# Two key chunks for every query block of the neighbourhood heads, and P transposed by full banks

## Chip, core and metric

The kernel runs on one core of one Trainium2 chip. The metric is device time in microseconds (us) for one execution, the median of the runs shown. Engines: PE is TensorE, DVE VectorE, ACT ScalarE, POOL GpSimd, SP the engine that issues most loads.

## What is computed

A trunk of two layers over 512 tokens of 1024 features, in float32. Each layer projects the normalised input once into queries, keys, values and gates, runs two kinds of attention, gates and projects both, adds the result to x, and adds a SwiGLU block (hidden width 2816). The attention part of a layer, cut:

```
qa, ka, va, qb, kb, vb, ga, gb = split(rms_norm(x) @ w_in)
ya = window_gqa(rope(norm(qa)), rope(norm(ka)), va, sink) @ w_proj_a      # 8 heads, 2 key heads
yb = neighbourhood_attn(norm(qb), norm(kb), vb, rel_bias) @ w_proj_b      # 8 heads
x  = x + (sigmoid(ga) * ya + sigmoid(gb) * yb) @ w_out
```

The **first kind** of head (window) lets a token see tokens at most 128 away, plus a sink in the softmax's sum. The **second kind** (neighbourhood) treats the 512 tokens as a grid of 8 rows by 64 columns. A query sees all 8 rows, and in each row the 16 columns around its own (clipped at the edge), with a bias from a table by row and column distance.

## The kernel before

Matrix products are done in three parts, high by high, high by low and low by high, with every float32 operand split into two float32r halves. PE work comes from two places. The main stream (`layer`, lines 1146 on) issues the projections in order: query, key/value, the second kind's q/k and v, the gates, and from line 1362 the output projections, which first ask for `head15`. Between its matmuls it yields, and a planner (`issue`, `drive`, lines 393 to 419) lets small generators, the chains, issue one step when a model of the engines' clocks says that the step's data will be there. This order is fixed when the program is built. On the chip each engine runs its own instructions in that order, and a step whose data is late holds up all that stands behind it on its engine. All engine calls pass through one helper, so nearly every row of the profile says L309. Scratch tiles come from arenas that a packer fills; a tile can be written only when the tile that lay there before is done with.

Each kind has 8 heads a layer, so 32 heads in all, and each head runs `head` (lines 1010 to 1091):

- For each of four blocks of 128 queries, scores in a bank of 512 columns, "at": one matmul with the high and one with the low half of the keys. Keys are held in four chunks of 128. Block j takes chunks j-1 to j+1 as far as they exist (`span`, `width`), so 256 columns for blocks 0 and 3 and 384 for 1 and 2, ten blocks of 128 by 128 in all. DVE adds mask or bias and finds the maximum, ACT takes the exponential and its sum.
- DVE or ACT scales by the reciprocal of the sum.
- Four steps, one for each key chunk in the order 1, 0, 2, 3 (`CHUNKS`): two or three transposes of 128 by 128 into a bank, ACT copies the high half, DVE subtracts to get the low half, and two matmuls add values times P^T into an output bank. Chunk 1 comes first and opens the bank: its two matmuls run over all 512 columns, with a zeroed last quarter in its buffers (`ptw`, zeroed in `chain_rope_tables`, lines 782 to 802). The other chunks use 256 or 384 columns.

For the second kind tokens are held by column blocks: a block of 128 is 16 grid columns by 8 rows (`by_columns`, `held`), and queries are turned with a reversed identity (`rev`), so that one table slice serves as bias. `chain_pair_b` (lines 1244 to 1271) runs a pair of these heads: `bias_load` issues 8 small loads a head on SP, `q_parts` and `k_parts` turn and split queries and keys, and `k_parts` issues four moves between partitions on SP, two for each head. Then each head waits for its bias, and `bias_mask` adds the mask in three DVE instructions. A pair begins when the bias of the pair before has been added.

Small inputs are issued at the start (lines 707 to 728), x on SP, the rest on POOL: positions, four gain loads, weight slab 1, two gains of the first kind, slab 2, the constants (masks and frequencies), slab 3, the sinks. `first_load` issues slabs 0 to 3 of the query projection. `chain_tables` (lines 744 to 777) first copies positions and negates the sinks on DVE, then uses the constants.

Of the kernel before, what the change touches and what calls it, by code (L numbers as in the profile page):

```python
# [13 lines left out]
F32R = mybir.dt.float32r  # L14
# [5 lines left out]
P = 128  # L20
# [40 lines left out]

C_ID, C_REV, C_MA, C_MB, C_INV, C_W = 0, 128, 256, 640, 752, 784


def constants():

    c = np.zeros((P, C_W), np.float32)
    i = np.arange(P)
    c[i, C_ID + i] = 1.0
    c[i, C_REV + P - 1 - i] = 1.0  # L70
    q, k = i[:, None], i[None, :]
# [3 lines left out]
    qc = 15 - (i % 16)[:, None]  # L75
    kc = np.arange(16)[None, :]
    at = C_MB
    for jb, ds in ((0, (0, 1)), (1, (-1, 0, 1)), (3, (-1, 0))):
        qcol = 16 * jb + qc
        cs = np.clip(qcol - 8, 0, 48)  # L80
        for d in ds:
            kcol = 16 * (jb + d) + kc
            c[:, at : at + 16] = np.where((kcol >= cs) & (kcol < cs + 16), 0.0, NEG)
            at += 16
    c[:, C_INV : C_INV + 32] = np.array(INV_FREQ, np.float32)[None, :]
    return c
# [4 lines left out]
def by_columns(ap):  # L91

    return ap.rearrange("p (r cc c) -> p cc r c", cc=NB, r=8)


def held(ap):
    return ap.rearrange("p (cc r c) -> p cc r c", cc=NB, r=8)

# [115 lines left out]
def trunk(ctx: ExitStack, tc: tile.TileContext, a: dict, out: bass.AP, lay: Layout):  # L214
# [10 lines left out]
    def nm(s):  # L225
        uid[0] += 1
        return f"{s}_{uid[0]}"
# [21 lines left out]
    def act(dtype=F32):  # L249
        return buf([S], dtype)  # L250
# [435 lines left out]
    ident = cst[:, C_ID : C_ID + P]  # L686
    rev = cst[:, C_REV : C_REV + P]
    maskA = cst[:, C_MA : C_MA + 3 * P]
    vec = cp.tile([32, P], F32, tag="vec", name="vec")
# [21 lines left out]
    for c in range(KD):  # L711
        x_load(c)
    posi = cp.tile([P, P], I32, tag="posi", name="posi")
    GQ.dma_start(
        posi[64:68].rearrange("q (r c) -> q r c", c=16), a["positions"].rearrange("(r cc c) -> cc r c", cc=NB, r=8)
    )
    for i, n in enumerate(("q_norm_b", "k_norm_b")):
# [12 lines left out]
    A.copy(warm, ones)  # L730
# [51 lines left out]
    def chain_rope_tables(l):  # L782
        yield Need(keys=["trig"])
        tabs.clear()
        ptw.clear()
        for i in range(4):
            ptw.append(act(F32R))
            V.tensor_scalar(ptw[i][:, 3 * P :], ident, 0.0, None, ALU.mult)
        for i, scale in enumerate((HD ** -0.5, 1.0)):
# [173 lines left out]

    def q_parts(tiles, col, perm, res, scale=None):

        yield Need("pe", tiles, [at_slots])
        ps = turned(tiles, col, perm)
# [37 lines left out]

    ptw = []
    CHUNKS = (1, 0, 2, 3)
    LAST_USE = {0: (0,), 2: (1,), 3: (2, 3)}

    def head(g, q, k, v, bias, perm, init, sink, o_dst, in_a, key):  # L1010

        kh, kl = k
        m = sp.tile([P, NB], F32, tag="negm", name=nm("negm"), bufs=4)
        den = sp.tile([P, NB], F32, tag="den", name=nm("den"), bufs=4)
        pr = []
        for j in range(NB):
            yield Need("pe", [q, kh, kl], [at_slots, sb_slots])
            lo, n = P * span(j)[0], width(j)
            at_slots.take()
            sb_slots.take()  # L1020
            ps = at_bank()
            mm(ps[:, :n], q[:, P * j : P * j + P], kh[:, lo : lo + n], True, False)
            mm(ps[:, :n], q[:, P * j : P * j + P], kl[:, lo : lo + n], False, True)
            sb = buf([3 * P])
            pr.append(sb)
            yield Need("dve", [ps])
            V.tensor_tensor_reduce(
                sb[:, :n], ps[:, :n], bias(j), -1.0, init, ALU.add, ALU.min, m[:, j : j + 1]
            )
            at_slots.give(clock["dve"])  # L1030
            yield Need("act", [sb])
            A.activation(
                sb[:, :n], sb[:, :n], AF.Exp, bias=m[:, j : j + 1], scale=-1.0, accum_out=den[:, j : j + 1]
            )
        done.add(f"{key}scores{g}")
# [8 lines left out]
        for j in range(NB):  # L1044
            n = width(j)
            yield Need("any", [rec])
            if lay.choose(lambda: clock["act"] + 0.2 < clock["dve"]):
                A.activation(pr[j][:, :n], pr[j][:, :n], AF.Copy, scale=rec[:, j : j + 1])
            else:
                V.tensor_scalar(pr[j][:, :n], pr[j][:, :n], rec[:, j : j + 1], None, ALU.mult)  # L1050
        po = None
        for i, c in enumerate(CHUNKS):
            jl, jh = span(c)
            n = width(c)
            yield Need("pe", pr[jl : jh + 1], [at_slots] + ([] if c == 1 else [th_slots]))
            at_slots.take()
            pt = at_bank()
            for j in range(jl, jh + 1):
                x = P * (c - span(j)[0])
                T.transpose(pt[:, P * (j - jl) : P * (j - jl) + P], pr[j][:, x : x + P], perm)  # L1060
            for j in LAST_USE.get(c, ()):
                sb_slots.give(clock["pe"])
            yield Need("act", [pt])
            if c == 1:
                th, tl = ptw[2 * (g % 2)], ptw[2 * (g % 2) + 1]
            else:
                th_slots.take()
                th = buf([3 * P], F32R)
                tl = buf([3 * P], F32R)
            yield from gsplit(pt[:, :n], th[:, :n], tl[:, :n])  # L1070
            at_slots.give(clock["dve"])
            yield Need("pe", [th, tl, v], [at_slots] if c == 1 else [])
            if c == 1:
                at_slots.take()
                po = at_bank()
                o, n = po, S
            else:
                o = po[:, P * jl : P * jl + n]
            mm(o, v[:, c, :], th[:, :n], c == 1, False)
            mm(o, v[:, c, :], tl[:, :n], False, i == NB - 1)  # L1080
            if c != 1:
                th_slots.give(clock["pe"])
        done.add(f"{key}products{g}")
# [9 lines left out]
    def bias_load(l, h):  # L1093

        t = buf([8, 48])
        src = a["rel_bias_b"]
        base = (l * 8 + h) * 15 * BW
        for r in range(8):
            Q.dma_start(
                t[16 * r : 16 * r + 16],  # L1100
                bass.AP(tensor=src.tensor, offset=base + r * BW, ap=[[1, 16], [BW, 8], [1, 48]]),
            )
        return t

    def bias_mask(t):

        bm = buf([7, 8, 16])
        for i, n, d in ((0, 2, 0), (2, 3, -1), (5, 2, -1)):
            m = cst[:, C_MB + 16 * i : C_MB + 16 * (i + n)].rearrange("p (d c) -> p d c", c=16)
            b = t[:, :, 16 * (d + 1) : 16 * (d + 1 + n)].rearrange("p r (d c) -> p d r c", c=16)  # L1110
            V.tensor_tensor(bm[:, i : i + n], b, m.unsqueeze(2).to_broadcast([P, n, 8, 16]), ALU.add)

        def of(j):
            i, n = {0: (0, 2), 3: (5, 2)}.get(j, (2, 3))
            return bm[:, i : i + n].rearrange("p d w c -> p (d w c)")

        return of

# [27 lines left out]
    def layer(l):  # L1146
# [68 lines left out]
        def chain_pair_a(hp):  # L1215
# [3 lines left out]
            qs = []  # L1219
            yield from q_parts(qa, P * hp, ident, qs)  # L1220
            oa.append(act())
# [22 lines left out]
        def chain_pair_b(hp):  # L1244
# [8 lines left out]
            qs, ks = [], []  # L1253
            yield from q_parts(raw, col, rev, qs, scale=gb[:, l : l + 1])
            yield from k_parts(raw, 4 * HD + col, ident, ks)
# [405 lines left out]
```

## Time and profile before

| | |
|---|---|
| median of 3 runs | 1417.02 us (1416.55 to 1417.68) |
| profiled execution, time | 1418.54 us |
| its span, first to last instruction | 1416.8 us |
| PE, DVE, ACT busy | 98%, 66%, 50% of the span |
| mean granted TensorE clock | 0.997 |

Times in the profile count from the start of the span. An engine's busy time is the union of its instructions' durations. A matmul's duration reaches into the next one's, so the mean duration is longer than the distance from one start to the next. Idle time is shown with what released the engine. The granted clock of 1.00 is 2.4 GHz, that of 0.50 is 1.2 GHz.

### The profile page before, as it was taken

To read this page: it belongs to the slowest core of one execution; us is meant where nothing else is said; L and a number is where in the kernel's file an instruction comes from. 1 tells how busy PE (TensorE), PEld (TensorE's weight loads), DVE (VectorE), ACT (ScalarE), POOL (GpSimd) and SP (SyncE) were. 2 spreads that over 40 slices of the span, in tenths; PEclk is the share of its full clock that TensorE was granted. 3 is DMA by queue.
4 is the path that set the end of the run, shared out by engine and by line. 5 is a ranking of instruction groups with operands and counts; after the bars stand their busy time and mean duration, and the time that the engine had idled before them with its cause. 6 is when DMAs were issued, how large, how long until landed. Compare 5 with 4: busy or idle time off the path is not lost.

```text
span 1416.8 us, 20995 instructions
## 1 busy us (share of the span) xinstructions
PE 1392.4 (98%) x8074; PEld 1221.9 (86%) x8074; DVE 934.1 (66%) x1768; ACT 711.6 (50%) x1209; POOL 316.3 (22%) x325
## 2 busy tenths in 40 slices
PE   7999999999999999999999999999999999999998
PEld 5778888888899999999987888888888999999997
DVE  4877788545777566575648868774559657565653
ACT  5476766643554344333544776665347433343441
POOL 3533222220121111101244322223002210111110
PEclk9999999999999999999999999999999999999999
DMA  7877789795486564735799677989657583745545
GB/s 194 156 157 131 141 154 167 142 232 149 90 173 154 120 141 130 177 89 127 138 198 187 128 141 145 160 156 189 145 163 129 125 203 95 179 106 133 134 90 119
DMA packets 197300, 208.49 MB, mean 147 GB/s; under 512 B 25533, under 2 KB 167025, under 8 KB 197201
## 3 DMA queue, kind: packets, MB, share of 16 engines
q0 software_dynamic: 134944, 141.53, 53.9%
q1 hardware_dynamic: 61904, 65.09, 15.8%
q8 instruction: 63, 1.03, 0.3%
q10 hardware_dynamic: 352, 0.54, 0.1%
q14 instruction: 37, 0.30, 0.1%
HBM read 194.55 MB, written 2.10 MB: 139 GB/s over the span
## 4 chain that ended last, share of the span: by engine, by line
PE 86%; DVE 9%; ACT 3%; DMA 1%; issue 1%; POOL 0%; DVEq 0%; ACTq 0%; POOLq 0%
PE mm L309 66%; PE at L309 20%; DVE arena L309 6%; DVE sm L309 3%; ACT arena L309 2%; DMA snk<-in_sink_a 1%; DMA vec<-in_q_norm_b 0%; ACT L309 0%; DVE hf L309 0%; DVE den L309 0%; ACT mm L309 0%; ACT sm L309 0%; POOL posi L309 0%; POOL arena L309 0%; DVEq L1656 0%
## 5 line engine op out<-in xcount | busy, mean ns | idle before, releaser
L309 PE MATMUL mm<-arena 128*128 128x512 f32 (+1 forms) x5568 | 1125.2, 357 | 7.4 <-DVE arena L309 4.6
L309 PEld LDWEIGHTS mm<-arena 128*128 128x128 f32 x5568 | 904.6, 190 | 140.3 <-DVE arena L309 7.0
L309 ACT CAST arena<-arena 128x1024 fp32r<-128x1024 f32 (+2 forms) x278 | 235.4, 870 | 207.3 <-DVE arena L309 196.1
L309 PE MATMUL at<-arena 128*128 128x256 f32 (+2 forms) x1952 | 301.4, 295 | 1.8 <-DVE arena L309 1.5
L309 DVE TENSOR_TENSOR arena<-arena,arena 128x1024 fp32r<-128x1024 f32 (+2 forms) x268 | 262.0, 993 | 59.7 <-ACT arena L309 59.4
L309 PEld LDWEIGHTS at<-arena 128*128 128x128 f32 x1952 | 265.0, 191 | 20.7 <-DVE arena L309 5.1
L309 ACT ACTIVATE arena<-arena 128x1024 fp32r<-128x1024 f32 (+3 forms) x252 | 207.5, 843 | 140.4 <-DMA arena<-in_w_down 70.4
L309 DVE TENSOR_TENSOR arena<-arena,mm 128x512 f32<-128x512 f32 x144 | 98.8, 686 | 231.9 <-PE mm L309 231.9
L309 POOL DMA_DIRECT2D arena<-in_w_in x163 | 161.8, 1387 | 343.1 <-ACT arena L309 331.5
L309 POOL DMA_DIRECT2D arena<-in_w_down x96 | 98.1, 1220 | 501.1 <-ACT arena L309 346.2
L309 DVE TENSOR_TENSOR arena<-arena 128x1024 f32<-128x1024 f32 (+4 forms) x196 | 158.4, 823 | 2.3
L309 DVE TENSOR_TENSOR arena<-at,arena 128x384 fp32r<-128x384 f32 (+4 forms) x206 | 114.8, 562 | 62.1 <-ACT arena L309 55.7
L309 ACT CAST arena<-at 128x384 fp32r<-128x384 f32 (+2 forms) x164 | 74.6, 459 | 106.3 <-PE at L309 92.3
L309 PE MATMUL at<-cst,arena 128*128 128x128 f32 x504 | 86.1, 277 | 5.0 <-DVE arena L309 4.0
L309 PEld LDWEIGHTS at<-cst,arena 128*128 128x128 f32 x504 | 64.3, 142 | 22.4 <-DVE arena L309 6.8
L309 ACT ACTIVATE arena<-arena,negm 128x256 f32<-128x256 f32 (+1 forms) x128 | 71.5, 560 | 16.7 <-DVE negm L309 15.9
L309 ACT COPY arena<-at 128x512 f32<-128x512 f32 (+1 forms) x68 | 39.5, 581 | 63.4 <-PE at L309 63.1
L309 DVE TENSOR_TENSOR arena<-mm,arena 128x512 f32<-128x512 f32 x72 | 49.3, 686 | 22.5 <-PE mm L309 22.2
L309 DVE CUSTOM_DVE_ANT_0 arena<-at,cst,nsnk 128x256 f32<-128x256 f32 (+1 forms) x64 | 34.5, 545 | 20.1 <-PE at L309 19.9
L309 ACT ACTIVATE arena<-arena,vecT 128x512 fp32r<-128x512 f32 x24 | 17.4, 726 | 55.0 <-DVE arena L309 54.6
L309 DVE CUSTOM_DVE_ANT_0 arena<-at,arena 128x256 f32<-128x256 f32 (+1 forms) x64 | 30.7, 486 | 8.9 <-PE at L309 8.4
L309 POOL DMA_DIRECT2D arena<-in_w_up x8 | 8.2, 1031 | 125.2 <-PE mm L309 77.6
(69 smaller groups left out, 429.3 us busy)
## 6 DMA issues: line engine op xcount, KB each, us to landing
arena<-in_w_in POOLq DMA_DIRECT2D x99, 512.0 KB, 7.2
arena<-in_w_down POOLq DMA_DIRECT2D x80, 512.0 KB, 6.7
arena<-in_w_gate SPq DMA_DIRECT2D x20, 1024.0 KB, 7.1
arena<-in_w_up SPq DMA_DIRECT2D x20, 1024.0 KB, 5.1
arena<-in_w_in POOLq DMA_DIRECT2D x64, 256.0 KB, 6.1
arena<-in_w_proj_a POOLq DMA_DIRECT2D x16, 512.0 KB, 7.2
arena<-in_w_proj_b POOLq DMA_DIRECT2D x16, 512.0 KB, 7.1
arena<-in_w_out SPq DMA_DIRECT2D x16, 512.0 KB, 6.4
```

The source lines that it names most:

```text
L309: f(*args, **kw)
```

## The change

- **Blocks of 8 columns shifted by half.** For the second kind a chunk of 128 tokens is now ordered by groups of 8 grid columns (`by_columns`, `held` with c=8). A query block lies across two key chunks: the outermost groups of both edges form block 0, which takes key chunks 0 and 3 (read as two runs of 128 by `keys_b`); the other three blocks take two neighbouring chunks. So every block has 256 score columns, eight blocks of 128 by 128. `turned_back` turns the queries accordingly; its first transpose writes two runs of 64 columns with a doubled reversed identity `rev2`.
- **Bias.** `bias_load` issues 16 loads a head, each with 64 pieces of 128 bytes, in place of 8 with 128 pieces of 192 bytes. `bias_mask` keeps three DVE instructions, over 512 columns in place of 896.
- **P^T by full banks.** The steps of both kinds are written out in tables. `STEPS_A` has three steps of 512, 384 and 384 columns, `STEPS_B` two of 512. A step transposes, splits, and multiplies for one or two chunks; no product is padded, and the zeroed buffers go. Every step takes one of two buffers for its halves. Two transposes of a second-kind head write two runs of 64.
- **Order at the start.** Positions come in two loads; slabs 2 and 3 are issued ahead of the first kind's gains, and the constants last.

```diff
 def by_columns(ap):
-    return ap.rearrange("p (r cc c) -> p cc r c", cc=NB, r=8)
+    return ap.rearrange("p (r cc c) -> p cc r c", r=8, c=8)
...
+    for h in range(2):
+        GQ.dma_start(
+            posi[64:68, 64 * h : 64 * h + 64].rearrange("q (r c) -> q r c", c=8),
+            a["positions"].rearrange("(r q h c) -> h q r c", q=NB, h=2, r=8)[h],
+        )
...
+    gains_b(0, "q_norm_b")
     first_load(1)
+    gains_b(1, "k_norm_b")
+    first_load(2)
+    first_load(3)
     gqa = cp.tile([P, 2, DEPTH, HD], F32, tag="gqa", name="gqa")
...
-    first_load(2)
-    GQ.dma_start(cst[:, P:], a["consts"][:, P:])
-    first_load(3)
...
     GQ.dma_start(snk, a["sink_a"].rearrange("l h -> (l h)").unsqueeze(0).to_broadcast([P, DEPTH * 8]))
+    GQ.dma_start(cst[:, P:], a["consts"][:, P:])
...
+    STEPS_A = (
+        (
+            [turn_a(0, 0, 0), turn_a(0, 1, P), turn_a(3, 2, 2 * P), turn_a(3, 3, 3 * P)],
+            S, [(0, slice(0, 256), slice(0, 256)), (3, slice(256, S), slice(256, S))], (),
+        ),
+        ([turn_a(1, j, P * j) for j in range(3)], 384, [(1, slice(0, 384), slice(0, 384))], (0,)),
+        ([turn_a(2, j, P * j - P) for j in range(1, 4)], 384, [(2, slice(0, 384), slice(P, S))], (1, 2, 3)),
+    )
+    STEPS_B = (
+        (
+            [(0, 0, 0), (3, 0, slice(64, 192)), (0, P, 256), (1, P, slice(320, 448))],
+            S, [(0, slice(0, 256), slice(0, 256)), (3, slice(256, S), slice(256, S))], (0,),
+        ),
+        (
+            [(3, P, slice(0, P)), (2, 0, slice(P, 256)), (2, P, slice(256, 384)), (1, 0, slice(384, S))],
+            S, [(1, slice(0, 256), slice(64, 320)), (2, slice(256, S), slice(192, 448))], (1, 2, 3),
+        ),
+    )
+    def keys_b(k, j):
+        if j:
+            return k[:, P * (3 - j) : P * (5 - j)]
+        return k.rearrange("p (c n) -> p c n", n=P)[:, 0::3, :]
...
-        for i, c in enumerate(CHUNKS):
-            jl, jh = span(c)
-            n = width(c)
-            yield Need("pe", pr[jl : jh + 1], [at_slots] + ([] if c == 1 else [th_slots]))
+        for i, (turns, n, products, ends) in enumerate(steps_):
+            yield Need("pe", [pr[t[0]] for t in turns], [at_slots, th_slots])
...
-            mm(o, v[:, c, :], th[:, :n], c == 1, False)
-            mm(o, v[:, c, :], tl[:, :n], False, i == NB - 1)
+            for c, cols, to in products:
+                mm(po[:, to], v[:, c, :], th[:, cols], i == 0 and c == 0, False)
+                mm(po[:, to], v[:, c, :], tl[:, cols], False, i == len(steps_) - 1 and c == products[-1][0])
...
-        for r in range(8):
-            Q.dma_start(
-                t[16 * r : 16 * r + 16],
-                bass.AP(tensor=src.tensor, offset=base + r * BW, ap=[[1, 16], [BW, 8], [1, 48]]),
+        for half in range(2):
+            for r in range(8):
+                p = 64 * half + 8 * r
+                Q.dma_start(
+                    t[p : p + 8],
+                    bass.AP(tensor=src.tensor, offset=base + r * BW + 8 * half, ap=[[1, 8], [BW, 8], [1, 32]]),
+                )
```

## Rows read from the trace of the kernel before

**Rows 1.** The page's first part: busy us, share of the span, instructions.

```profile
PE 1392.4 (98%) x8074; PEld 1221.9 (86%) x8074; DVE 934.1 (66%) x1768; ACT 711.6 (50%) x1209; POOL 316.3 (22%) x325
```

**Rows 2.** The chain that ended last, shares of the span by engine.

```profile
PE 86%; DVE 9%; ACT 3%; DMA 1%; issue 1%; POOL 0%; DVEq 0%; ACTq 0%; POOLq 0%
```

**Rows 3.** Windows: length, busy PE PEld DVE ACT POOL, granted clock, DMA share, GB/s.

```profile
50.00:175.00 125.00, 122.61 (x627) 101.95 (x626) 95.62 (x297) 79.21 (x179) 44.67 (x46) 1.00 0.79 147
175.00:275.00 100.00, 99.68 (x526) 84.13 (x525) 76.96 (x198) 65.07 (x149) 24.97 (x25) 1.00 0.86 156
```

**Rows 4.** The same chain in order of time: start, us, what (merged).

```profile
277.92 95.91 PE mm L309 x423
...
402.39 2.88 PE at L309 x24
```

**Rows 5.** Timeline of PE, 200 to 206 us: start, us to last end, what.

```profile
203.32 0.60 PE L309 MATMUL at<-cst,arena 128*128 128x128 f32 x4
203.68 0.48 PE L309 MATMUL at<-arena 128*128 128x256 f32 x2
204.00 0.85 PE L309 MATMUL mm<-arena 128*128 128x512 f32 x3
```

**Rows 6.** Groups by shape, PE: count, busy us, mean ns, idle before.

```profile
L309 PE MATMUL at<-cst,arena 128*128 128x128 f32 x504 | 86.1, 277 | 5.0 <-DVE arena L309 4.0 <-issue 0.7
L309 PE MATMUL at<-arena 128*128 128x384 f32 x192 | 51.0, 354 | 1.0 <-DVE arena L309 0.7
L309 PE MATMUL at<-arena 128*128 128x512 f32 x64 | 20.4, 400 | 0.0
```

**Rows 7.** Timeline of SP: three trains of bias loads, and the start of two.

```profile
171.01 9.66 SPq L309 DMA_DIRECT2D arena<-in_rel_bias_b  x16
...
193.64 12.10 SPq L309 DMA_DIRECT2D arena<-in_rel_bias_b  x16
...
225.13 11.01 SPq L309 DMA_DIRECT2D arena<-in_rel_bias_b  x16
...
171.01 3.74 SPq L309 DMA_DIRECT2D arena<-in_rel_bias_b  x8
...
225.13 6.17 SPq L309 DMA_DIRECT2D arena<-in_rel_bias_b  x11
```

**Rows 8.** Timeline of PE: the first scores of second-kind pairs two to four.

```profile
199.12 0.28 PE L309 MATMUL at<-arena 128*128 128x256 f32 x1
...
220.56 0.40 PE L309 MATMUL at<-arena 128*128 128x256 f32 x2
...
248.25 0.37 PE L309 MATMUL at<-arena 128*128 128x256 f32 x1
```

**Rows 9.** DMA issues (median us to landing), and the bias table's landings.

```profile
arena<-arena SPq DMA_DIRECT2D x40, 128.0 KB, 4.5
...
DMA to landing us min/median/max: 1.8/4.5/7.0
```

**Rows 10.** Timeline of POOL, DVE and PE, 8 to 23 us; idle before in brackets.

```profile
8.89 0.56 POOL L309 DMA_DIRECT2D cst<-in_consts  x1 [2.05 <-DMA vec<-in_q_norm_b]
...
10.15 0.56 POOL L309 DMA_DIRECT2D snk<-in_sink_a  x1
...
20.15 0.18 DVE L309 TENSOR_SCALAR nsnk<-snk 128x16 f32<-128x16 f32 x1 [7.37 <-DMA snk<-in_sink_a]
...
22.50 0.67 DVE L309 TENSOR_SCALAR arena<-cst,vec2T 128x32 f32<-128x32 f32 x4
...
20.97 1.46 PE L309 MATMUL mm<-arena 128*128 128x512 f32 x2 [3.95 <-DVE arena L309]
```

**Rows 11.** Windows of the start, columns as in rows 3.

```profile
15.00:20.00 5.00, 2.02 (x10) 1.28 (x8) 0.00 (x0) 1.93 (x4) 0.00 (x0) 1.00 1.25 329
20.00:25.00 5.00, 4.03 (x11) 3.08 (x12) 4.06 (x12) 1.65 (x3) 0.00 (x0) 0.50 0.36 79
25.00:30.00 5.00, 5.00 (x21) 4.04 (x21) 3.54 (x10) 3.37 (x6) 2.74 (x3) 0.82 0.29 36
```

More of the change, by code (lines that the diff above doesn't have):

```diff
@@ L70, in constants @@
     c[i, C_REV + P - 1 - i] = 1.0
+    c[:, C_REV + P : C_REV + P + 64] = c[:, C_REV : C_REV + 64]
     q, k = i[:, None], i[None, :]
@@ L73, in constants @@
     c[:, C_MA + 2 * P : C_MA + 3 * P] = np.where(k <= q, 0.0, NEG)
[L75 to L84, printed above, removed]
+    half, qcol = (i // 64)[:, None], (23 - 8 * (i // 64) - i % 8)[:, None]
+    kc = np.arange(32)[None, :]
+    c[:, C_MB : C_MB + 32] = np.where((kc >= qcol - 8) & (kc < qcol + 8), 0.0, NEG)
+    c[:, C_MB + 32 : C_MB + 64] = np.where(kc // 16 == half, 0.0, NEG)
     c[:, C_INV : C_INV + 32] = np.array(INV_FREQ, np.float32)[None, :]
@@ L91, in by_columns @@
 def by_columns(ap):
-    return ap.rearrange("p (r cc c) -> p cc r c", cc=NB, r=8)
+    return ap.rearrange("p (r cc c) -> p cc r c", r=8, c=8)
 def held(ap):
-    return ap.rearrange("p (cc r c) -> p cc r c", cc=NB, r=8)
+    return ap.rearrange("p (cc r c) -> p cc r c", r=8, c=8)
 class Layout:
@@ L687, in trunk @@
     rev = cst[:, C_REV : C_REV + P]
+    rev2 = cst[:, C_REV + 64 : C_REV + 64 + P]
     maskA = cst[:, C_MA : C_MA + 3 * P]
@@ L713, in trunk, with gains_b @@
     posi = cp.tile([P, P], I32, tag="posi", name="posi")
[L714 to L717, printed above, removed]
+    for h in range(2):
[3 more added lines that the diff above has]
+        )
+    def gains_b(i, n):
         for h in range(2):
             GQ.dma_start(vec2[2 * i : 2 * i + 2, HD * h : HD * h + HD], a[n])
+    gains_b(0, "q_norm_b")
     first_load(1)
+    gains_b(1, "k_norm_b")
+    first_load(2)
+    first_load(3)
     gqa = cp.tile([P, 2, DEPTH, HD], F32, tag="gqa", name="gqa")
@@ L962, in turned, with turned_back, q_parts @@
         return ps
-    def q_parts(tiles, col, perm, res, scale=None):
+    def turned_back(tiles, col):
+        at_slots.take()
+        ps = at_bank()
+        for b in range(NB):
+            t = tiles[b][:, col : col + P]
+            if b:
+                T.transpose(ps[:, 448 - P * b : 576 - P * b], t, rev)
+            else:
+                T.transpose(ps.rearrange("p (a n) -> p a n", n=64)[:, 0::7, :], t, rev2)
+        return ps
+    def q_parts(tiles, col, res, scale=None):
         yield Need("pe", tiles, [at_slots])
-        ps = turned(tiles, col, perm)
+        ps = turned(tiles, col, ident) if scale is None else turned_back(tiles, col)
         for own, other in HALVES:
@@ L1003, in width, with turn_a, keys_a @@
         return P * (hi - lo + 1)
-    ptw = []
-    CHUNKS = (1, 0, 2, 3)
-    LAST_USE = {0: (0,), 2: (1,), 3: (2, 3)}
+    def turn_a(c, j, to):
+        return j, P * (c - span(j)[0]), slice(to, to + P)
+    STEPS_A = (
[20 more added lines that the diff above has]
+        return k.rearrange("p (c n) -> p c n", n=P)[:, 0::3, :]
+    def keys_a(k, j):
+        lo = P * span(j)[0]
+        return k[:, lo : lo + width(j)]
     def head(g, q, k, v, bias, perm, init, sink, o_dst, in_a, key):
         kh, kl = k
+        steps_, keys = (STEPS_A, keys_a) if in_a else (STEPS_B, keys_b)
         m = sp.tile([P, NB], F32, tag="negm", name=nm("negm"), bufs=4)
@@ L1017, in head @@
             yield Need("pe", [q, kh, kl], [at_slots, sb_slots])
-            lo, n = P * span(j)[0], width(j)
+            n = width(j) if in_a else 2 * P
             at_slots.take()
@@ L1021, in head @@
             ps = at_bank()
[L1022 to L1024 removed]
+            mm(ps[:, :n], q[:, P * j : P * j + P], keys(kh, j), True, False)
+            mm(ps[:, :n], q[:, P * j : P * j + P], keys(kl, j), False, True)
+            sb = buf([n])
             pr.append(sb)
             yield Need("dve", [ps])
[L1027 to L1029 removed]
+            V.tensor_tensor_reduce(sb, ps[:, :n], bias(j), -1.0, init, ALU.add, ALU.min, m[:, j : j + 1])
             at_slots.give(clock["dve"])
             yield Need("act", [sb])
[L1032 to L1034 removed]
+            A.activation(sb, sb, AF.Exp, bias=m[:, j : j + 1], scale=-1.0, accum_out=den[:, j : j + 1])
         done.add(f"{key}scores{g}")
@@ L1051, in head @@
         po = None
-        for i, c in enumerate(CHUNKS):
-            jl, jh = span(c)
-            n = width(c)
-            yield Need("pe", pr[jl : jh + 1], [at_slots] + ([] if c == 1 else [th_slots]))
+        for i, (turns, n, products, ends) in enumerate(steps_):
+            yield Need("pe", [pr[t[0]] for t in turns], [at_slots, th_slots])
             at_slots.take()
+            th_slots.take()
             pt = at_bank()
[L1058 to L1061, printed above, removed]
+            for j, x, to in turns:
+                if isinstance(to, int):
+                    T.transpose(pt[:, to : to + 256].rearrange("p (a n) -> p a n", n=64)[:, 0::3, :], pr[j][:, x : x + P], rev2)
+                else:
+                    T.transpose(pt[:, to], pr[j][:, x : x + P], perm)
+            for j in ends:
@@ L1062, in head @@
                 sb_slots.give(clock["pe"])
             yield Need("act", [pt])
[L1064 to L1070, printed above, removed]
+            th, tl = buf([n], F32R), buf([n], F32R)
+            yield from gsplit(pt[:, :n], th, tl)
             at_slots.give(clock["dve"])
-            yield Need("pe", [th, tl, v], [at_slots] if c == 1 else [])
@@ L1073, in head @@
-            if c == 1:
+            yield Need("pe", [th, tl, v], [at_slots] if po is None else [])
+            if po is None:
                 at_slots.take()
                 po = at_bank()
-                o, n = po, S
-            else:
-                o = po[:, P * jl : P * jl + n]
-            mm(o, v[:, c, :], th[:, :n], c == 1, False)
-            mm(o, v[:, c, :], tl[:, :n], False, i == NB - 1)
-            if c != 1:
-                th_slots.give(clock["pe"])
+            for c, cols, to in products:
+                mm(po[:, to], v[:, c, :], th[:, cols], i == 0 and c == 0, False)
+                mm(po[:, to], v[:, c, :], tl[:, cols], False, i == len(steps_) - 1 and c == products[-1][0])
@@ L1083, in head @@
+            th_slots.give(clock["pe"])
         done.add(f"{key}products{g}")
@@ L1093, in bias_load @@
     def bias_load(l, h):
-        t = buf([8, 48])
+        t = buf([8, 32])
         src = a["rel_bias_b"]
-        base = (l * 8 + h) * 15 * BW
-        for r in range(8):
-            Q.dma_start(
-                t[16 * r : 16 * r + 16],
-                bass.AP(tensor=src.tensor, offset=base + r * BW, ap=[[1, 16], [BW, 8], [1, 48]]),
-            )
+        base = (l * 8 + h) * 15 * BW + 8
+        for half in range(2):
[5 more added lines that the diff above has]
+                )
         return t
     def bias_mask(t):
[L1107 to L1117, printed above, removed]
+        bm = buf([2, 2, S // 4])
+        for i, n, k0 in ((0, 2, 0), (2, 1, 1), (3, 1, 0)):
+            o = bm.rearrange("p e k (a n) -> p (e k a) n", n=64)[:, 2 * i : 2 * (i + n)]
+            m = cst[:, C_MB + 16 * i : C_MB + 16 * (i + n)].rearrange("p (d c) -> p d c", c=8)
+            b = t[:, :, 16 * k0 : 16 * (k0 + n)].rearrange("p r (d c) -> p d r c", c=8)
+            V.tensor_tensor(
+                o.rearrange("p d (r c) -> p d r c", c=8), b, m.unsqueeze(2).to_broadcast([P, 2 * n, 8, 8]), ALU.add
+            )
+        return lambda j: bm[:, int(j == 0)].rearrange("p k n -> p (k n)")
     def mask_a(j):
@@ L1219, in chain_pair_a @@
             qs = []
-            yield from q_parts(qa, P * hp, ident, qs)
+            yield from q_parts(qa, P * hp, qs)
             oa.append(act())
@@ L1253, in chain_pair_b @@
             qs, ks = [], []
-            yield from q_parts(raw, col, rev, qs, scale=gb[:, l : l + 1])
+            yield from q_parts(raw, col, qs, scale=gb[:, l : l + 1])
             yield from k_parts(raw, 4 * HD + col, ident, ks)
```

11 lines of the change are left out of this document (3 added, 8 removed).

## The prediction

> **What bounds the kernel now.** I began with the page's busy line: TensorE (PE) is busy 1392.4 of 1416.8 us, 98%, while VectorE (DVE) has 66% and ScalarE (ACT) 50% [rows 1]. "Busy" can hide stalls, so the chain that ended last came next: 86% of it is PE's own work, 9% DVE, 3% ACT, 1% a transfer [rows 2]. Then the windows, to see where in a layer PE has idle time at all. While the first layer's heads run (50 to 275 us) it misses 2.39 and 0.32 us [rows 3]. Behind them, from 277.92 on, 95.91 us of the chain are 423 gate matmuls without a break [rows 4], and only then does the program ask for the last head. So a head that finishes later costs nothing by itself, within some 90 us. What costs time is PE's in-order queue: PE work taken out of the heads shortens the span one for one, and a head instruction that reaches the front of PE's queue before its data is there lengthens it one for one. The second layer repeats this.
>
> **Prices of PE work.** A matmul's listed duration (354 ns at 384 columns [rows 6]) overlaps its neighbour's, so I priced by spacing. 24 of 256 columns fill 2.88 us, 0.120 each; 423 of 512 fill 95.91, 0.227 each [rows 4]. For 384 columns the middle of the two is 0.173; I take 0.175. In one stretch of a head four transposes and two matmuls of 256 columns lie between 203.32 and 204.00: (0.68 - 0.24) / 4 = 0.11 for a transpose [rows 5]. The counts agree with the code: 64 matmuls of 512 columns into "at" are two for each of 32 heads, the 192 of 384 are four for scores and two for products [rows 6].
>
> **The change, part by part.**
> Second kind, 16 heads in both layers. Scores: four matmuls go from 384 to 256 columns, 4 x 0.055 = 0.22 us. Transposes of P: ten become eight, 0.22 us. Products: two of 512 and two of 384 become four of 256, 2 x 0.107 + 2 x 0.055 = 0.324 us. Together 0.764 us a head, 12.2 us in all.
> First kind, 16 heads: ten transposes stay ten; the two products padded to 512 columns give way so that two of 384 stand in their place, 2 x 0.052 = 0.104 us a head, 1.7 us in all.
> PE sum: 13.9 us less, all of it on the path, since PE is the bound wherever heads run.
>
> The Trainium skill, "TensorE: Matmul & The Clock Gate", Part 4 (PE-mode transpose), gives about 275 ns for a transpose in one kernel's context. The mean duration of one, 277 ns [rows 6], agrees, but the spacing does not [rows 5]; by the page's figure the 32 transposes that go would be worth 8.8 us where I count 3.5.
>
> Splits, exponentials, bias adds: fewer and narrower on ACT and DVE. I price them at nothing, because PE's 99.68 of 100 us covers ACT's 65.07 and DVE's 76.96 [rows 3]; were the cover gone, they would be a gain, not a cost. The zeroed buffers (four small DVE instructions a layer) likewise.
>
> Strided operands: the first block's keys are read as two runs, and 40 transposes (two a head, one a pair) write two runs of 64. No row has such an operand on PE. Bounds: nothing, or double time, 32 x 0.120 + 40 x 0.11 = 8.2 us. The nearest rows are plain operands of the same width [rows 4, 5], and the runs of 64 and 128 are long; I take nothing.
>
> Steps of a head: three and two in place of four, the first of them waiting for all four blocks. Fewer hand-overs could return part of the 2.39 + 0.32 us a layer that PE idles [rows 3], 5.4 at most; other hand-overs could cost as much. I take 0.
>
> SP's queue. Each pair of second-kind heads now issues 32 small bias transfers, not 16, and the pair's four key moves (128 KB each) queue behind them on SP. A train of 16 took 9.66, 12.10 and 11.01 us [rows 7]. The first scores of these pairs start at 199.12, 220.56 and 248.25 and need the second move, which lands 4.5 us after issue [rows 8, 9]. So its issue must come by 194.6, 216.1 and 243.75. With trains that start at 171.01, 193.64, 225.13 and 0.5 us for the first move, a train may last 23.1, 21.9 and 18.1 us before PE waits. How long do 32 last? At best as the first eight of a train do, 3.74 / 8 = 0.47 each [rows 7]: 15 us, no wait. At worst eight in flight wait for the longest landing, 7.0 us [rows 9], 0.875 each: 28 us, waits of 4.9 + 6.1 + 9.9 = 20.9 a layer, 42 in all. The row nearest to a long train is 11 issues in 6.17 us, 0.56 each [rows 7]; each transfer also has half the pieces it had (64, of 128 bytes). So 17.9 us. With heads about 1.5 us a pair shorter the last pair's margin falls to 16.6: 1.3 us a layer, **2.6 us lost**.
>
> The start. DVE stands 7.37 us for the sinks, and PE 3.95 us behind it; then the clock, full before, is granted at 0.50, the lower level of 1.2 GHz, from 20 to 25 us and at 0.82 on average to 30 [rows 10, 11]. The sinks were issued on POOL at 10.15, behind slab 3 and the constants (8.89). Now positions take two issues in place of one, the slabs come earlier and the constants go last: the sinks stay twelfth, with one 328 KB transfer less ahead. But POOL already stalled 2.05 us at the constants for an earlier transfer to land, and that wait now sits ahead of other issues; behind it wait the constants, which DVE needs at 22.50, and the next weights. Bounds: the whole stall and its slow clock go, 3.95 + half of the 5.8 us from 20.97 to the clock's return (0.82 over 25 to 30 puts that at 26.8) = 6.9 us; or the constants become the late one: last in the queue, behind a wait like the 2.05 us one, they keep DVE standing some 2 us longer at 22.50 (an estimate). I take what one transfer less is worth, 328 KB at the 329 GB/s of 15 to 20 us: **1.0 us gained**.
>
> **Sum.** 13.9 - 2.6 + 1.0 = 12.3 us. The profiled execution took 1418.54 us (span 1416.8 and 1.7 around it): 1406.2. The median of the runs, 1417.02, is 1.5 lower, so 1404.7.
>
> **Rivals.**
> *SP sets the pace of the second-kind heads (slower).* If a train lasts well over 18 us, PE stands at the scores of every pair. For: at the old mean of 0.68 us (10.9 for 16) a train of 32 takes 21.8 us, PE stalls 3.7 a layer, and the time is 1409.5. It decides near 24 us, 0.75 an issue, where some 9 us a layer eat the gain; at the worst bound the time is 1444. Against: half the pieces, and a train that ends earlier than its moves are ready costs nothing. Chance 0.14, half of it within no change, half slower.
> *The start frees itself.* The sinks land before PE runs dry, the clock stays up: 5.9 us more gain, 1398.8. For: one transfer less ahead. Against: DVE still waits at the same instruction. Chance 0.12.
> *Strided operands run at half rate.* 8.2 us back: 1412.9. Only the missing row speaks for it. Chance 0.05.
> *A transpose holds PE for its 277 ns.* 5.3 us more gain, 1399.4. The spacing speaks against it [rows 5]. Chance 0.01. The Trainium skill's page of that section states a figure of this size.
> The forecast keeps 0.68.
>
> **How the numbers follow.** The low end takes the start's 6.9 us in full and no SP loss: 1417.0 - 20.8 = 1396. The high end takes SP at the old rate (7.4 lost) and 2 us of a worse start, or the strided price: 1413. Below and above lie about 2 in 10. About 0.2%, 2.8 us, is what a measurement of this kernel can tell from no change. Faster: forecast, start, strided and transpose cases, 0.86; same 0.07; slower 0.07.
>
> **What the changed profile would show.** Right: "at" matmuls of 512 columns gone, those of 384 down from 192 to 128, the transposes from 504 to 472; spacings unchanged; no PE idle time put down to a key move. Wrong: PE idle before 256-column "at" matmuls released by a transfer; trains over 23 us on SP; the strided transposes spaced wider than 0.11 us; a longer DVE wait before 25 us.

## The result: slower, and the profile after

The changed kernel took 1422.86 us (median of 20 runs, 1414.66 to 1424.89) beside 1417.57 (20 runs, 1415.81 to 1418.00): ratio 1.0037, 95% interval [1.0029, 1.0044]. The forecast was 1404.7, range 1396 to 1413. It was wrong in its sign.

First the busy line of the page, for the kernel before [rows 1] and here, and the span:

```profile
span 1420.9 us, 20923 instructions
...
PE 1382.4 (97%) x8042; PEld 1215.2 (86%) x8042; DVE 915.3 (64%) x1720; ACT 697.5 (49%) x1153; POOL 317.3 (22%) x326
```

TensorE (PE) is busy 10.0 us less, as a cut in its work should have it. But its idle time, span less busy, went from 1416.8 - 1392.4 = 24.4 us to 38.5. The groups by shape tell which instructions the idle time stands before (last number: idle us and what ended it):

```profile
L305 PE MATMUL at<-arena 128*128 128x256 f32 x1824 | 257.5, 287 | 18.7 <-DMA arena<-arena 14.8 <-DVE arena L305 2.1 <-ACT arena L305 1.4
...
L305 PE MATMUL at<-cst,arena 128*128 128x128 f32 x472 | 75.6, 279 | 4.9 <-DVE arena L305 4.2 <-DMA arena<-in_x 0.2 <-DVE negm L305 0.2
L305 PE MATMUL at<-arena 128*128 128x384 f32 x128 | 34.1, 350 | 0.0
```

The counts are those forecast [rows 6]. New is "DMA arena<-arena 14.8": PE stands at scores of 256 columns until a key move has landed. The windows place it (columns as in rows 3):

```profile
50.00:175.00 125.00, 122.02 (x633) 102.22 (x632) 92.88 (x276) 80.56 (x177) 41.01 (x42) 1.00 0.81 150
175.00:275.00 100.00, 92.23 (x485) 77.78 (x484) 67.57 (x180) 56.95 (x126) 22.92 (x23) 0.95 0.77 142
```

From 175 to 275 us PE misses 7.77 us where it missed 0.32 [rows 3], and its granted clock, 1.00 before, is 0.95 on average. PE's timeline there, and in the second layer, has two gaps each (in brackets: idle us before, and what ended it):

```profile
216.46 0.58 PE L305 MATMUL at<-arena 128*128 128x256 f32 x1 [3.81 <-DMA arena<-arena]
220.36 0.58 PE L305 MATMUL at<-arena 128*128 128x256 f32 x1 [3.32 <-DMA arena<-arena]
...
911.22 0.39 PE L305 MATMUL at<-arena 128*128 128x256 f32 x1 [2.69 <-DMA arena<-arena]
916.56 0.58 PE L305 MATMUL at<-arena 128*128 128x256 f32 x1 [4.96 <-DMA arena<-arena]
```

It is the third pair of second-kind heads, in both layers. SP's timeline tells why its moves were late (start, us, what):

```profile
189.71 19.62 SPq L305 DMA_DIRECT2D arena<-in_rel_bias_b  x32
211.02 4.28 SPq L305 DMA_DIRECT2D arena<-arena  x4
215.35 15.83 SPq L305 DMA_DIRECT2D arena<-in_rel_bias_b  x32
235.21 5.17 SPq L305 DMA_DIRECT2D arena<-arena  x4
```

The pair's 32 bias loads hold SP until 209.33, its first move goes out at 211.02, and PE had come to the scores at 216.46 - 3.81 = 212.65. The chain of waits shows the second move:

```profile
211.58 8.73 DMA arena<-arena
220.31 0.04 issue
220.36 0.58 PE at L305
```

It landed 8.73 us after its issue, against a median of 4.5 [rows 9]. Behind the gaps the clock was low. These two windows are cut at the granted clock's fall and return in each layer:

```profile
216.18:226.42 10.24, 6.64 (x23) 5.77 (x24) 2.50 (x8) 2.19 (x8) 0.00 (x0) 0.50 0.54 91
912.50:922.70 10.20, 6.14 (x22) 5.56 (x23) 2.50 (x8) 2.27 (x8) 0.00 (x0) 0.50 0.57 90
```

For some 10 us in each layer PE ran at a granted 0.50, the lower level of 1.2 GHz. The fall comes while PE stands, at the end of the first gap in the first layer and early in the second gap in the other. The start is better than forecast; DVE's wait for the sinks [rows 10], and the window in which the clock had been 0.50 [rows 11]:

```profile
16.50 0.17 DVE L305 TENSOR_SCALAR nsnk<-snk 128x16 f32<-128x16 f32 x1 [3.72 <-DMA snk<-in_sink_a]
```

```profile
20.00:25.00 5.00, 5.00 (x26) 3.97 (x25) 4.79 (x13) 4.92 (x8) 2.74 (x3) 1.00 0.20 24
```

So two gains came, and something near 20 us went to the third pair's moves. The runs below test that and split it.

### The profile page after: what moved, and what is told of

Its sections match the earlier page's. It is cut to its first block, busy times and chain, and to the rows that moved or that the text cites. A ratio compares the mean times of both kernels' runs of the same rounds, so it can differ in the third digit from the quotient of the medians.

```text
span 1420.9 us, 20923 instructions
## 1 busy us (share of the span) xinstructions
PE 1382.4 (97%) x8042; PEld 1215.2 (86%) x8042; DVE 915.3 (64%) x1720; ACT 697.5 (49%) x1153; POOL 317.3 (22%) x326
## 3 DMA queue, kind: packets, MB, share of 16 engines
q1 hardware_dynamic: 61904, 64.04, 15.4%
## 4 chain that ended last, share of the span: by engine, by line
PE 79%; DVE 11%; ACT 4%; DMA 3%; issue 2%; POOL 0%; SPq 0%; DVEq 0%; ACTq 0%; POOLq 0%
PE mm L305 62%; PE at L305 18%; DVE arena L305 8%; ACT arena L305 4%; DVE sm L305 2%; DMA arena<-arena 1%; DMA arena<-in_rel_bias_b 1%; DMA vec<-in_q_norm_b 0%; DMA arena<-in_w_in 0%; DMA snk<-in_sink_a 0%; SPq L305 0%; DVE hf L305 0%; POOL posi L305 0%; ACT sm L305 0%; ACT mm L305 0%
## 5 line engine op out<-in xcount | busy, mean ns | idle before, releaser
L305 PE MATMUL at<-arena 128*128 128x256 f32 (+1 forms) x1952 | 288.7, 291 | 18.7 <-DMA arena<-arena 14.8
L305 DVE TENSOR_TENSOR arena<-at,arena 128x512 fp32r<-128x512 f32 (+4 forms) x158 | 103.1, 659 | 29.1 <-ACT arena L305 23.9
L305 ACT CAST arena<-at 128x512 fp32r<-128x512 f32 (+2 forms) x116 | 64.0, 553 | 99.6 <-PE at L305 84.7
L305 PE MATMUL at<-cst,arena 128*128 128x128 f32 x472 | 75.6, 279 | 4.9 <-DVE arena L305 4.2
L305 ACT ACTIVATE arena<-arena,negm 128x256 f32<-128x256 f32 (+1 forms) x128 | 68.2, 534 | 13.4 <-DVE negm L305 12.5
L305 PEld LDWEIGHTS at<-cst,arena 128*128 128x128 f32 x472 | 58.2, 143 | 17.5 <-DVE arena L305 5.7
L305 DVE CUSTOM_DVE_ANT_0 arena<-at,arena 128x256 f32<-128x256 f32 x64 | 26.3, 420 | 30.3 <-PE at L305 30.0
L305 DVE TENSOR_SCALAR arena<-arena,sm 128x256 f32<-128x256 f32 (+1 forms) x106 | 35.9, 397 | 1.1
```

What stands on the lines that cost most here:

```text
L305: f(*args, **kw)
```

## Experiments

**One bias table a pair.** The changed kernel with 16 loads a pair in place of 32; odd heads use the table of the head before, so their own is left out.

```diff
-            rb = [bias_load(l, 2 * hp + i) for i in range(2)]
+            rb = [bias_load(l, 2 * hp)] * 2
```

> The changed kernel, but both heads of a second-kind pair use the bias table of the first, so a pair issues 16 small loads on SP, not 32. Theory A (the train): in the changed kernel the key moves of the third pair stand behind a train of 32 loads, PE waits for them 7 to 8 us a layer, and its clock drops for the next 10 us. With 16 loads PE idle time put down to key moves falls from 14.8 us to under 1 us, the clock stays at full speed from 50 us on, and the time is 1400 to 1406 us. Theory B (the heads): the scores come too early for their key moves because the heads are shorter and are planned closer together, whatever SP has to issue. Then most of the idle time stays and the time is above 1415 us.

1402.99 us, ratio to before 0.9898 [0.9883, 0.9913]. SP's timeline at the third pair:

```profile
189.63 10.59 SPq L305 DMA_DIRECT2D arena<-in_rel_bias_b  x16
201.72 4.97 SPq L305 DMA_DIRECT2D arena<-arena  x4
207.33 10.74 SPq L305 DMA_DIRECT2D arena<-in_rel_bias_b  x16
```

The train starts where it did, ends 9 us earlier, and the moves go out from 201.72; the first still waits 1.4 us for a bias load to land, the others for ACT and DVE, that is for their data. No PE idle time is put down to a key move, and the clock is 1.00 from 175 to 275 us. PE work, operands and steps are those of the changed kernel, so the loads ahead of the moves cost it 20 us.

**Two pairs ahead.** All loads kept; each train is issued two pairs early.

```diff
+            for n in ((0, 1) if hp == 0 else ()):
+                tables[n] = [bias_load(l, 2 * n + i) for i in range(2)]
+            rb = tables[hp]
...
             yield from k_parts(raw, 4 * HD + col, ident, ks)
+            if hp < 2:
+                tables[hp + 2] = [bias_load(l, 2 * hp + 4 + i) for i in range(2)]
```

> The changed kernel with all its loads, but the tables of a pair are issued two pairs earlier: the first two trains before the first pair's key moves, the third behind them, the fourth behind those of the second pair. Theory A: the third pair's train goes out in the 13 us in which SP stood idle, its moves are issued when they are ready, PE idle for key moves is under 1 us and the time is 1400 to 1406 us. Theory B: as above, over 1415 us. A third view (contention: the moves land late because weights arrive at the same time) also gives over 1415 us, with landings of the moves above 5 us and PE still waiting.

1419.01 us (10 runs, 1413.21 to 1422.51), ratio 1.0006 [0.9990, 1.0023]. A miss, and SP's timeline tells why:

```profile
152.61 18.90 SPq L305 DMA_DIRECT2D arena<-in_rel_bias_b  x32
186.37 3.57 SPq L305 DMA_DIRECT2D arena<-arena  x4
190.00 18.41 SPq L305 DMA_DIRECT2D arena<-in_rel_bias_b  x32
209.37 27.57 SPq L305 DMA_DIRECT2D arena<-arena  x8
```

Now the fourth pair's train fills 190 to 208 us, and the third pair's moves stand behind that one, issued from 209.37. PE still waits 10.9 us for moves, 7.27 of it at one place in the second layer. Whose loads they are doesn't matter; what lies ahead of that pair's moves does.

**The kernel before with 32 loads.** Each load of 16 partitions is cut into two of 8, as the change has them; the pieces, and all of PE's work, stay.

```diff
-            Q.dma_start(
-                t[16 * r : 16 * r + 16],
-                bass.AP(tensor=src.tensor, offset=base + r * BW, ap=[[1, 16], [BW, 8], [1, 48]]),
-            )
+            for s in range(2):
+                Q.dma_start(
+                    t[16 * r + 8 * s : 16 * r + 8 * s + 8],
+                    bass.AP(tensor=src.tensor, offset=base + r * BW + 8 * s, ap=[[1, 8], [BW, 8], [1, 48]]),
+                )
```

> The kernel before, with each bias load cut into two of 8 partitions, so that a pair issues 32 loads of 64 pieces. Theory A: trains of 15 to 20 us as in the changed kernel; against the margins of 23, 22 and 18 us in the old timeline that costs 0 to 2.5 us a layer, so 1417 to 1424 us, and PE idle time put down to key moves appears. Theory B: no such idle time, 1416.5 to 1418.5 us.

1426.49 us, ratio 1.0065 [1.0050, 1.0080], more than either theory gave. The number of loads alone costs the old kernel 9.5 us. There it is the fourth pair that is late, the one the prediction had found to have the least room:

```profile
222.39 17.66 SPq L309 DMA_DIRECT2D arena<-in_rel_bias_b  x32
241.40 4.13 SPq L309 DMA_DIRECT2D arena<-arena  x4
```

```profile
246.72 0.35 PE L309 MATMUL at<-arena 128*128 128x256 f32 x1 [0.97 <-DMA arena<-arena]
249.88 1.23 PE L309 MATMUL at<-arena 128*128 128x256 f32 x3 [2.80 <-DMA arena<-arena]
```

**The kernel before, cut by key rows.** Again 32 loads, but each covers 16 partitions with half the rows.

```diff
...
+                    t[16 * r : 16 * r + 16, 4 * s : 4 * s + 4],
+                    bass.AP(tensor=src.tensor, offset=base + (r + 4 * s) * BW, ap=[[1, 16], [BW, 4], [1, 48]]),
...
```

> The kernel before, each of a head's eight loads cut in two by key rows instead of by partitions: 32 loads a pair as in the run that cut them by partitions, but each still covers 16 partitions, with 4 pieces each in place of 8. Theory: the time of a train goes with the number of loads, by the 0.55 us that one took there; then trains of 14 to 18 us again, PE waits for key moves of some 8 us in all, and 1424 to 1428 us. Rival: a load of 8 partitions is slow because its pieces go to half of the sixteen DMA engines; a load of 16 partitions with half the pieces each then takes about half the time that it took before, trains come out at 9 to 13 us as in the kernel before, no PE wait for moves over 1 us, and 1416 to 1419 us.

1435.49 us, ratio 1.0129 [1.0114, 1.0144], with 11.7 us of PE waiting for moves. The rival falls: with as many pieces in all, a train takes longer still. The third and fourth train of the first layer:

```profile
193.67 20.80 SPq L309 DMA_DIRECT2D arena<-in_rel_bias_b  x32
...
226.13 21.90 SPq L309 DMA_DIRECT2D arena<-in_rel_bias_b  x32
```

One load's issue has a median of 424 ns here and 304 ns in the run before. The 1435.49 was above what that theory gave (1424 to 1428), so the price of a load is not one number.

**The start, put into the kernel before.**

```diff
+    gains_b(0, "q_norm_b")
     first_load(1)
+    gains_b(1, "k_norm_b")
+    first_load(2)
+    first_load(3)
...
-    first_load(2)
-    GQ.dma_start(cst[:, P:], a["consts"][:, P:])
-    first_load(3)
...
+    GQ.dma_start(cst[:, P:], a["consts"][:, P:])
```

> The kernel before with only the order of the first POOL issues of the changed one (slabs 2 and 3 ahead of the first kind's gains, constants last). If the order of issues is what moved the start, DVE waits about 3.7 us for the sinks and not 7.4, the clock does not drop between 20 and 30 us, and the time falls by about 6 us, to 1411 to 1412.5. If the rest of the change moved the start, it stays within 2 us of 1417.5.

1413.36 us, ratio 0.9974 [0.9963, 0.9984]: 3.6 us gained, less than the 6 expected. In the profiled execution, the longest of the eight (1415.36 us), DVE waits 4.72 us for the sinks in place of 7.37 [rows 10], and the clock is still 0.74 on average from 20 to 25 us.

**The start, taken out of the changed kernel.** The inverse edit.

> The changed kernel with the start's loads on GpSimd in their old order (constants ahead of the last two gain loads and of the sinks). Theory: the start alone is worth 3.6 us in the kernel before (measured with the order of after put into it) to 6 us (what the two traces show), and the rest of the change doesn't depend on it: 1426 to 1429 us, VectorE again waiting for the sinks at about 20 us. Rival: the start's gain is lost again later in the changed kernel (the heads wait for transfers in any case): within 1.5 us of the changed kernel, 1421.5 to 1424.5.

1426.74 us, 1.0070 [1.0055, 1.0085]: 3.9 us more than the changed kernel, the same size from the other side. Its rival falls.

**Key moves on ACT's queue.** The loads stay on SP, so nothing stands ahead of the moves there.

```diff
-            Q.dma_start(kh[other].bitcast(F32), kh[own].bitcast(F32))
-            Q.dma_start(kl[other].bitcast(F32), kl[own].bitcast(F32))
+            AQ.dma_start(kh[other].bitcast(F32), kh[own].bitcast(F32))
+            AQ.dma_start(kl[other].bitcast(F32), kl[own].bitcast(F32))
```

> The changed kernel with the four key moves of a pair issued on ScalarE's queue; the 32 loads of a pair stay on SP's. Theory: the moves of the third pair were late because they stood behind the 32 loads in SP's order. They are then issued as soon as the keys are split, near 200 us, PE waits for no key move in the heads, the clock stays at full speed there, and the time is 1402 to 1407 us (1403.0 is what the run with one table a pair took; ScalarE's waiting for VectorE's half of a split may cost up to 4). Rival: the transfers themselves are slow to land beside so many small loads (8.7 us for the second move of the third pair), whatever queue they stand in: the moves still land 8 us and more after their issue, PE waits for them by 5 us and more, and the time is 1411 to 1420.

1423.52 us, ratio 1.0051 [1.0035, 1.0066]. Neither theory. PE's wait for moves is gone, but the tables come late in its place. Waits of DVE and ACT in the whole run, then of SP from 903 to 940 us (total us, times, longest):

```profile
DVE arena L305 <- DMA arena<-in_rel_bias_b: 12.0, 3, 7.0
...
ACT arena L305 <- DMA arena<-arena: 8.1, 2, 4.0
```

```profile
SPq L305 <- DMA arena<-arena: 17.9, 4, 7.8
SPq L305 <- DMA arena<-in_rel_bias_b: 5.4, 4, 2.9
```

In the second layer the fourth pair's loads go out between 909.27 and 937.70 us, 28 us for one train, because SP stands for key moves to land, 10.1 us in this train, though another engine issues them. The semaphores in the trace tell why: the transfers that SP and ACT issue share eight of them (100, 101 and 110 to 115), and each transfer waits until the one before on its semaphore has landed. The loads that SP held back until 926.15, 931.19 and 934.86 are on semaphores 100, 112 and 114, and the transfers before them there are the moves that ACT issued at 923.73, 926.64 and 927.22. PE then idles 6.13 us before transposes at 943.23.

**Tables three pairs ahead.** The first three trains when the first pair is prepared, the fourth behind that pair's moves.

```diff
+            for n in ((0, 1, 2) if hp == 0 else ()):
+                tables[n] = [bias_load(l, 2 * n + i) for i in range(2)]
+            rb = tables[hp]
...
+            if hp == 0:
+                tables[3] = [bias_load(l, 6 + i) for i in range(2)]
```

> The changed kernel, all of its 128 loads a layer kept and all on SP's queue, but issued at other places: those of the first three pairs together when the first pair is prepared, those of the fourth behind the first pair's key moves, where SP had 14 us of idle time. No train stands ahead of the second, third or fourth pair's moves. Theory (order in SP's queue): 96 loads take 52 to 64 us, before the heads of the second kind are due; the moves of the pairs 2 to 4 are issued in about 4 us each as soon as the keys are split, PE waits for no move, clock at full speed from 175 to 275 us, 1402 to 1406 us. Rival (the sheer number of loads is what costs, wherever they stand): PE waits for moves or tables move to the first and second pair, 1410 to 1420.

1424.03 us, ratio 1.0053 [1.0036, 1.0069]. In the first layer it is as expected: PE is busy 49.27 and 49.96 of 50 us in the windows from 175 and from 225, at a clock of 1.00. The second layer loses it all at one place; SP's and PE's timelines:

```profile
813.79 52.77 SPq L305 DMA_DIRECT2D arena<-in_rel_bias_b  x96
866.68 2.39 SPq L305 DMA_DIRECT2D arena<-arena  x4
```

```profile
868.93 1.28 PE L305 MATMUL at<-arena 128*128 128x256 f32 x2 [15.81 <-DMA arena<-arena]
```

There SP issues no load before 813.79 (from its last move, which ends at 758.65, it waits 47.3 us for DVE and 8.0 for PE), and 96 loads then stand ahead of the first pair's moves. The rule held, and I had placed the third train against it.

**Two trains moved.** The first two pairs' loads when the first pair is prepared, the third's behind the first pair's moves, the fourth's behind the third pair's. All loads kept, all on SP.

```diff
+            for n in ((0, 1) if hp == 0 else ()):
+                tables[n] = [bias_load(l, 2 * n + i) for i in range(2)]
+            rb = tables[hp]
...
+            for n in {0: (2,), 2: (3,)}.get(hp, ()):
+                tables[n] = [bias_load(l, 2 * n + i) for i in range(2)]
```

> The changed kernel with all of its loads on SP's queue, each train put where SP was idle or where the moves behind it are not due: those of the first two pairs when the first pair is prepared (64 loads, as in the run two pairs ahead), those of the third pair behind the first pair's moves (some 18 us, over before the second pair's moves are ready in both layers), those of the fourth behind the third pair's moves. Theory (order in SP's queue, with room enough ahead of each move): moves of the pairs 1 to 4 are issued as soon as the keys are split, the third pair's near 202 us, PE waits for no move over 1 us in either layer, no stretch at half clock from 175 to 275 us and in the second layer's heads, and 1402 to 1406 us, as the run with one table a pair (1403.0), faster than both kernels. Rival (the loads cost what they cost wherever they stand, as the two runs before this one came out at 1423.5 and 1424.0): a move or a table of another pair comes late, PE loses 8 us or more on it in one of the layers, 1411 to 1424.

1402.86 us (1402.29 to 1403.55), ratio 0.9900 [0.9883, 0.9916]: faster than both kernels, with the whole computation. SP's timeline and the busy line:

```profile
152.48 18.32 SPq L305 DMA_DIRECT2D arena<-in_rel_bias_b  x32
186.16 20.78 SPq L305 DMA_DIRECT2D arena<-arena  x8
206.99 19.70 SPq L305 DMA_DIRECT2D arena<-in_rel_bias_b  x32
226.80 3.88 SPq L305 DMA_DIRECT2D arena<-arena  x4
```

```profile
PE 1376.2 (98%) x8042; PEld 1209.8 (86%) x8042; DVE 914.2 (65%) x1720; ACT 697.7 (50%) x1153; POOL 317.4 (23%) x326
```

The trains shown are as long as ever, 18 to 20 us, but none keeps PE waiting. The eight moves of the second and third pair follow one another with no load between them. PE waits for no key move in either layer, and the mean clock is 1.000.

## Why the prediction was wrong, point by point

**PE work: right in its mechanism, 1.5 us too high.** The cleanest pair is the run with two trains moved against the old kernel with the new start, where PE waits for no move in either. Over the whole span PE's busy time is 1376.2 against 1390.9, 14.7 us less. But the two starts differ: from 20 to 25 us the clock is 1.00 in the one and 0.74 in the other. So I compare from a mark behind the start, the first matmul with the column of ones (tile `ones`), to the end: first the old kernel, then the changed one (columns as in rows 3).

```profile
39.74:1413.50 1373.76, 1359.81 (x7951) 1197.52 (x7949) 912.16 (x1712) 686.23 (x1169) 301.74 (x298) 1.00 0.70 146
37.64:1401.10 1363.46, 1347.40 (x7919) 1188.26 (x7917) 892.85 (x1668) 672.76 (x1113) 301.85 (x298) 1.00 0.70 146
```

PE has 32 fewer matmuls there and is busy 12.4 us less, where spacing gave 13.9. Counting 277 ns for each transpose would have given 5.3 more, 19.2. The means of one transpose (277 ns in either kernel) and of a 256-column "at" matmul (285 ns, 284 before) didn't move, and behind a matmul whose keys are two runs the next starts after 117 ns (median of 32), against 120 behind a plain one: the keys in two runs cost nothing that shows. Where the other 1.5 us went isn't shown. The Trainium skill, "TensorE: Matmul & The Clock Gate", Part 4 (PE-mode transpose), states about 275 ns in one kernel's context: as a duration the trace agrees, as a price to count with it does not.

**Steps of a head: taken as 0, a small loss.** In the same two windows idle time went from 1373.76 - 1359.81 = 13.95 us to 1363.46 - 1347.40 = 16.06, 2.1 more. The idle time before 256-column "at" matmuls went from 0.9 us to 4.0, put down to DVE and ACT. That is inside the bounds of 5.4 either way. Which hand-over costs it wasn't tried.

**The start: right in sign, mis-sized.** 1.0 us was taken; the medians gave 3.6 and 3.9, inside its bounds (6.9 gained to 2 lost). One trace doesn't size it: the first matmul with `ones` comes at 40.3 to 43.1 us in the four executions profiled with the old order, at 39.7 in the old kernel with the new order, and at 37.1 to 37.7 in the six of changed kernels with the new order. Whether their two loads of positions help there wasn't tried.

**SP's queue: the step that failed.** Its term was 2.6 us lost. The changed kernel and the version with two trains moved differ in the places of the loads alone: 1422.86 - 1402.86 = 20.0 us. In the profiles it is idle time, 38.5 - 24.9 = 13.6, and busy time, 1382.4 - 1376.2 = 6.2, which fits PE at its lower clock: in the two slow windows it is busy 6.64 + 6.14 = 12.78 us, and half of that is 6.4. The length of a train was not the mistake: the trains of pairs two to four took 20.28, 19.62, 15.83 us in the first layer and 17.28, 19.65, 15.02 in the second, mean 17.9, just the figure taken. Four things around it were wrong, all at the third pair:

- *The deadline.* The prediction gave that pair 21.9 us, from the old distance between train and scores, 220.56 - 193.64 = 26.9 [rows 7, 8]. Now it is 212.65 - 189.71 = 22.9, so 17.9 us were left for a train of 19.62. It let the heads shrink by 1.5 us a pair and charged that to the fourth pair only (the rival's 3.7 us a layer left out even that). The distance shrank by 4.0, in both layers alike, and mostly not by head work. These are PE's projections of 512 columns in the two stretches of the first layer, before and after:

```profile
L309 PE MATMUL mm<-arena 128*128 128x512 f32 x82 | 22.0, 400 | 0.0
...
L305 PE MATMUL mm<-arena 128*128 128x512 f32 x66 | 17.0, 396 | 0.0
```

  At 0.227 us each, 16 fewer are 3.6 us; head work is some 1.7 us less by the same spacings, and new idle time takes back 0.6. Both kernels have 3648 such matmuls in all, so the plan, made anew for the changed heads, put these 16 outside the stretch. They had been cover for the train. Why the plan moved them wasn't tried.
- *SP's wait for landings.* Between the last load (209.33) and the first move (211.02) lie 1.7 us; over the pair's train and moves SP waits 5.3 us for bias loads to land. The 0.5 us for the first move left that out. That move, on semaphore 101, went out when the load issued on the same semaphore at 204.86, eight issues earlier, had landed.
- *The landing.* 4.5 us was a median over the whole kernel; this move took 8.73. The old trace already had medians of 2.2, 6.2 and 5.7 us for the four moves of pairs two, three and four.
- *The clock.* A gap's price was taken as its length. Each layer's gaps brought 10.2 us at 0.50, and the 6.2 us of extra busy time come on top of the idle time.

The rival that SP sets the pace was the right one, with the wrong point: it decided not near trains of 24 us but at under 20, since the margin, not the train, had been misread. Its chance, 0.14, was too low for a term whose own bounds reached 42 us.

**The sum as measured.** Work and hand-overs -10.5 us by the medians (1402.86 against 1413.36; -12.4 + 2.1 in the traces), start -3.6, the third pair's moves +20.0: +5.9 in all, where the kernels differ by 1422.86 - 1417.57 = 5.3.

## What to carry to other kernels

When a change shortens a stage of the bound engine, lay out anew every deadline in it, from the new program's order and not from the old distances: a transfer hidden with a few us to spare becomes the bound once its cover is cut by as much, and the cover can be work that was only moved. In a queue that is served in order, put bulk loads behind the short transfers that an engine will wait for, or a stage earlier, in each layer and not in one alone; here moving two trains was worth 20 us, nearly four times what the change had lost. Price a gap on PE with the slow clock behind it, and a landing with those of its own stretch, not with a median over the kernel.

## What the runs showed of the hardware

A load's price on SP follows neither its bytes nor its pieces. With the same pieces, 16 loads took 9.66 to 12.10 us [rows 7], 32 of 8 partitions 13.87 to 18.53, and 32 of 16 partitions with half the rows 18.73 to 22.13. The page's packet counts show how the loads are spread: queue q1 counts 61904 packets in the kernel before, in that kernel with 32 loads a pair, and in the changed one, here:

```profile
q1 hardware_dynamic: 61904, 64.04, 15.4%
```

By rows it is 63952, 2048 more, which is 8 for each of 256 loads. That fits one closing packet from each DMA engine that a load uses: (64 + 8) x 256 = (128 + 16) x 128, and (64 + 16) x 256 is 2048 above both. One table a pair, 128 loads of 8 partitions, has 52688, which is (64 + 8) x 128 less, as it should be. By this reading a load of 8 partitions ran on 8 engines and one of 16 on 16. The Trainium skill, "DMA: Bandwidth & Descriptors", section "Why a DMA increments its semaphore by 16 and not by 1", says the same: the number of engines is the largest up to 16 that divides the slowest dimension of both sides. The counts agree. More engines did not make a train of small loads shorter, as the rival had it. One issue took longer with 16 partitions (median 424 ns with 64 pieces, 429 with the old kernel's 128) than with 8 (304 ns with 64 pieces), and the train with it.
